# Score tiles of 1024 keys over two PSUM banks in the attention stages of a hybrid block

## The chip, the cores and the metric

One core of one Trainium2 chip runs the whole layer. The metric is the device time of one execution in microseconds (us). Three runs of the kernel before took 2777.36, 2782.47 and 2783.66 us; their median is 2782.47.

## What is computed

One block of a residual trunk over 2048 rows of width 1024, in float32 at both ends: a normalised projection into six parts, differential attention (4 heads of two softmax maps) and stick-breaking attention (8 heads) beside each other, an output projection, and a gated feed-forward part. What the change touches are the two attentions:

```
def diff_attention(q, k, v, lam, rel_bias):       # per block of 128 queries
    logits = einsum('bqhcd,bkhcd->bhcqk', qb, k) * scale + bias     # c = 0, 1: two maps
    p = softmax(where(mask, logits, -inf))
    attn = p[:, :, 0] - lam * p[:, :, 1]
    return einsum('bhqk,bkhd->bqhd', attn, v)

def stick_breaking_attention(q, k, v):            # A[t,s] = beta_ts * prod_{s<j<t}(1 - beta_tj), s < t
    z = einsum('bqhd,bkhd->bhqk', qb, k) * scale
    log_1mb = where(mask, log_sigmoid(-z), 0)
    rem = cumsum(log_1mb, reverse=True) - log_1mb
    a = where(mask, exp(log_sigmoid(z) + rem), 0)
    return einsum('bhqk,bkhd->bqhd', a, v)
```

## The kernel before

The work is cut into 8 groups: groups 0 to 3 are the four heads of differential attention, groups 4 to 7 are pairs of stick-breaking heads. A stream of projections (`proj`, line 379, 16 row tiles a group) runs ahead of the attention of its group, under the attention of the group before, and after the last group comes the output projection (`out_proj`, line 744), which is interleaved with the end of group 7. The feed-forward part follows. `advance` (line 708) sets how far the projections are written ahead. The order of instructions on each engine is not written by hand: a scheduler picks, by priority and by when it expects operands and buffers to be free, and each engine then runs its own list in that order. The attention functions `probs` and `stage_a` have a raised priority (`"at": 200` in line 32).

Scores of a query block (128 queries, index i from 0 to 15) against its (i+1)*128 keys are made in blocks of up to 1024 keys (index b, so two blocks from i = 8 on), and these in pieces of up to 512 keys, the width of one PSUM bank. `score_chunk` (line 446) issues two matmuls per piece into a score tile `sc`, and for the diagonal a third one with a mask (line 450). The pool has four such tiles, one bank each (lines 478 and 552). Two further banks hold the value products `yp`, two the projections `pj`.

Differential attention (`probs`, line 462): for each of two maps m, VectorE copies a piece from PSUM to `z` with scaling and a running maximum (line 483), and for the last 256 keys with the bias added (line 487). Then follow exponentials on ScalarE (line 497), the difference of the maps on VectorE (line 507), and `split_t` (line 398), which splits the weights into two 16-bit halves (a cast and a subtraction, lines 89 or 93 and 98) and transposes them by DMA into `aT`, the input of the value matmuls (`pv`, line 453).

Stick-breaking attention (`stage_a`, line 540) goes through a block from its last piece to its first. For each piece ScalarE writes sigmoid(-z) to `om` (line 554) and sigmoid(z) over the scores in PSUM (line 555); VectorE scans the running product of `om` backwards (line 557), which names the PSUM tile as an operand too, and multiplies sigmoid(z) by the shifted product into `be` (line 558). Only then is the score tile free. A memset (line 545) or a copy of the carry of the block before (line 547) opens each block. `split_t` then casts `be` on ScalarE and subtracts on GpSimd. The profile names `om` and `be` both z. Value matmuls (`stage_b`, line 565) come up to five blocks later.

`transposed` (line 591) uses the same ring of score tiles for transposing rows at the start (line 611) and in the output path (line 782).

## Time and profile before

| | us |
|---|---|
| three runs | 2777.36, 2782.47, 2783.66 |
| profiled execution: span from its first to its last instruction | 2785.0 |
| differential attention (first to last score, some 106 to 616) | 510 |
| stick-breaking attention, first score of group 4 to last scan (616 to 1402) | 786 |
| output path and feed-forward, from some 1400 on | 1385 |

For the profiled execution the profile gives the span and no separate time around it; the span is 2.5 us over the median of the three runs and 1.3 us over the slowest. In rows of groups, a row has the line, engine and operation, the tiles out<-in, the count, then busy us and mean ns of one, then idle us of the engine just before such instructions, with what ended it. Rows of windows give start:end, length, and busy us with counts for PE, PE's weight loads (PEld), DVE (VectorE), ACT (ScalarE) and POOL (GpSimd), then the granted TensorE clock, the DMA share and GB/s.

### The profile page before, as it was taken

How to read it: one execution, taken by the hardware profiler on the slowest of the kernel's cores; microseconds unless marked ns; L12 is line 12 of the kernel's file. 1: busy time of each engine (PE TensorE's matmuls, PEld its weight loads, DVE VectorE, ACT ScalarE, POOL GpSimd, SP SyncE). 2: the span in 40 equal slices, each digit the busy share in tenths (PEclk: the TensorE clock that was granted, in tenths of full speed). 3: DMA queues.
4: the chain of work that ended last, by engine and by line, in shares of the span. 5: the costliest groups of instructions: out<-in, count | busy, mean ns of one | idle time of the engine just before them, and what ended most of it. 6: DMA issues, size and time to landing. Idle time of an engine off the chain costs nothing. (4 is left out here: it accounts for less than half of the span.)

```text
span 2785.0 us, 45469 instructions
## 1 busy us (share of the span) xinstructions
PE 2489.9 (89%) x17084; PEld 1409.0 (51%) x17084; DVE 2000.8 (72%) x3782; ACT 1361.8 (49%) x2543; POOL 1445.2 (52%) x1008
## 2 busy tenths in 40 slices
PE   6998989888878786888889798989999999999998
PEld 4665556555545453557775343444444444444443
DVE  6888879687989989876756877777786644434445
ACT  4665656466878788765644534443442212111121
POOL 2567767665544555546665656565654332322323
PEclk9999999999999897999999999999999999999999
DMA  6788787789999998997796565655658844635534
GB/s 225 199 167 184 147 188 163 164 174 205 198 205 198 192 182 160 190 198 205 197 309 253 184 235 189 221 187 191 240 170 299 327 155 178 227 125 190 211 129 166
DMA packets 649133, 551.91 MB, mean 198 GB/s; under 512 B 506624, under 2 KB 574208, under 8 KB 638672
## 3 DMA queue, kind: packets, MB, share of 16 engines
q1 hardware_dynamic: 647088, 546.92, 71.2%
q8 instruction: 134, 2.20, 0.3%
q0 software_dynamic: 512, 1.36, 0.2%
q10 hardware_dynamic: 1312, 0.72, 0.1%
q14 instruction: 87, 0.71, 0.1%
HBM read 265.27 MB, written 151.52 MB: 150 GB/s over the span
## 5 line engine op out<-in xcount | busy, mean ns | idle before, releaser
L98 POOL TENSOR_TENSOR s<-z,s 128x1024 f16<-128x1024 f32 (+7 forms) x288 | 474.1, 1654 | 334.8 <-ACT s L89 299.3
L320 PE MATMUL pj<-w,xt 128*128 128x384 f16 x3072 | 572.3, 334 | 32.6 <-DVE st L330 11.6
L320 PEld LDWEIGHTS <-xt 128*128 128x128 f16 x3072 | 299.9, 100 | 241.8 <-issue 36.3
L448 PE MATMUL sc<-kT,qT 128*128 128x512 f16 (+3 forms) x1280 | 346.9, 362 | 74.6 <-DVE z L558 34.4
L1034 PE MATMUL pd<-wd,act 128*128 128x512 f16 x1848 | 406.2, 379 | 3.3 <-DVE hs L1040 2.4
L557 DVE TENSOR_TENSOR_SCAN z<-z,sc 128x512 f32<-128x512 f32 (+3 forms) x320 | 355.5, 1112 | 68.6 <-ACT sc L555 65.1
L458 PE MATMUL yp<-v,aT 128*128 128x64 f16 (+1 forms) x4896 | 281.2, 207 | 80.0 <-DMA aT<-s 79.2
L458 PEld LDWEIGHTS <-aT 128*128 128x128 f16 x4896 | 245.2, 102 | 169.4 <-DMA aT<-s 105.1
L936 PEld LDWEIGHTS <-wg 128*128 128x128 f16 x1848 | 183.9, 100 | 264.3 <-issue 58.8
L98 POOL TENSOR_TENSOR hs<-hs,cu 128x512 f32<-128x512 f32 x132 | 170.5, 1297 | 238.2 <-DVE cu L1040 82.6
L936 PEld LDWEIGHTS <-wu 128*128 128x128 f16 x1848 | 181.0, 98 | 222.1 <-issue 9.0
L1034 PEld LDWEIGHTS <-act 128*128 128x128 f16 x1848 | 180.6, 98 | 222.6 <-issue 4.7
L98 POOL TENSOR_TENSOR act<-cg,act 128x512 f16<-128x512 f32 x117 | 160.8, 1385 | 247.7 <-ACT act L992 141.5
L98 POOL TENSOR_TENSOR fst<-fst 128x512 f32<-128x512 f32 x97 | 179.6, 1852 | 167.6 <-DVE wd L215 78.6
L1040 DVE SCALAR_TENSOR_TENSOR hs<-pd,c,hs 128x512 f32<-128x512 f32 x192 | 142.1, 748 | 160.8 <-PE pd L1034 159.1
L89 ACT CAST s<-z 128x384 f16<-128x384 f32 (+7 forms) x216 | 170.1, 788 | 151.5 <-DMA aT<-s 56.4
L554 ACT ACTIVATE z<-sc,c 128x512 f32<-128x512 f32 (+3 forms) x320 | 202.6, 633 | 10.6 <-PE sc L448 6.5
L558 DVE TENSOR_TENSOR z<-sc,z 128x512 f32<-128x512 f32 (+3 forms) x320 | 193.3, 606 | 8.1
L992 ACT CAST act<-cg 128x512 f16<-128x512 f32 x132 | 80.6, 617 | 234.2 <-DVE cg L998 190.9
L555 ACT ACTIVATE sc<-sc,c 128x512 f32<-128x512 f32 (+3 forms) x320 | 194.8, 609 | 0.0
L761 PE MATMUL po<-wo,mt 128*128 128x256 f16 x1536 | 181.3, 276 | 11.0 <-DVE xf L764 6.3
L936 PE MATMUL pm<-X,wg 128*128 128x512 f16 x792 | 179.1, 379 | 1.2 <-ACT bx L1109 1.2
(233 smaller groups left out, 4028.4 us busy)
## 6 DMA issues: line engine op xcount, KB each, us to landing
xt<-xs SPq DMA_DIRECT2D x112, 512.0 KB, 4.4
hs<-hd SPq DMA_DIRECT2D x96, 512.0 KB, 4.3
hd<-hs SPq DMA_DIRECT2D x80, 512.0 KB, 3.2
split<-wg SPq DMA_DIRECT2D x11, 1792.0 KB, 10.5
split<-wu SPq DMA_DIRECT2D x11, 1792.0 KB, 10.3
split<-wd SPq DMA_DIRECT2D x11, 1792.0 KB, 10.4
wg<-split SPq DMA_DIRECT2D x11, 1792.0 KB, 7.3
wd<-split SPq DMA_DIRECT2D x11, 1792.0 KB, 8.4
```

What stands on the lines that cost most here:

```text
L89: ACT.copy(dst, src)
L98: (DVE if e == "D" else POOL).tensor_tensor(dst, a_, b_, op)
L320: PE.matmul(pj[:, :384], lhsT=xv[:, xi, kt, :], rhs=G["w"][:, wi, kt, :], start=n == 0, stop=n == 23)
L448: PE.matmul(sc[:, : 128 * w].rearrange("p (t n) -> p t n", n=P), lhsT=G["q"][i // 4][:, 2 - 2 * o + m, i % 4, :], rhs=G["k"][q][:, m, 0:w, ...
L458: PE.matmul(yp[:, y0 : y0 + wd], lhsT=aT[:, a_, :], rhs=v[:, v_ : v_ + wd], start=start and j == 0 and q == 0, stop=stop and j == nb - 1 a ...
L554: ACT.activation(om[:, lo:hi], sc[:, :w], AF.Sigmoid, scale=G["nkz"][:])
L555: ACT.activation(sc[:, :w], sc[:, :w], AF.Sigmoid, scale=G["kz"][:])
L557: DVE.tensor_tensor_scan(ov, ov, sc[:, :w], om[:, hi : hi + 1], op0=ALU.mult, op1=ALU.bypass)
L558: DVE.tensor_tensor(be[:, lo:hi], sc[:, :w], om[:, lo + 1 : hi + 1], ALU.mult)
L761: PE.matmul(po[:, sl], lhsT=mt[:, kt, P * xi : P * xi + P], rhs=wos[2 * h + n][wi][:, kt, :], start=q == 0, stop=q == 23)
L936: PE.matmul(ps_[:].rearrange("p (t n) -> p t n", n=P), lhsT=wv[:, wo, wi, 128 * kt : 128 * kt + 128], rhs=X[xo][:, :, xi, kt, :], start=st ...
L1034: PE.matmul(po[:], lhsT=act[:, ao, xi, 128 * j : 128 * j + 128], rhs=W["d"][:, wo, wi, :], start=start and u == 0 and q == 0, stop=u == nu ...
```

## The change

The four score tiles of 512 keys become two of 1024 keys, over two banks each (`scores`, a new function of one line). Each piece's matmuls still write one bank. The instructions behind them run once over all keys of a block, up to 1024: in differential attention the scaling with maximum and the biased one, in stick-breaking the two sigmoids, the scan and the product. `transposed` takes a whole two-bank tile and uses its first half. Cut to its core:

```
+            def scores():
+                return ps.tile([P, 1024], F32, tag="sc", bufs=2, name=nm("sc"))
...
-                            z = z4()
+                            z, sc = z4(), scores()
                             for c in range((n + 511) // 512):
                                 lo, hi = 512 * c, min(512 * c + 512, n)
-                                sc = ps.tile([P, 512], F32, tag="sc", bufs=4, name=nm("sc"))
-                                score_chunk(G, sc, i, 2 * b + c, m, (hi - lo) // P)
-                                f = min(max(near - 1024 * b - lo, 0), hi - lo)
-                                note("D", 1.05 * (hi - lo) + 200)
-                                if f > 0:
-                                    DVE.tensor_scalar(z[:, lo : lo + f], sc[:, :f], ...)
...
+                                score_chunk(G, sc[:, lo:hi], i, 2 * b + c, m, (hi - lo) // P)
+                            f = min(max(near - 1024 * b, 0), n)
+                            note("D", 1.05 * n + 200)
+                            if f > 0:
+                                DVE.tensor_scalar(z[:, :f], sc[:, :f], ...)
...
+                            if f < n:
+                                DVE.tensor_tensor_reduce(z[:, f:n], sc[:, f:n], ...)
...
+                    sc = scores()
                     for c in range((n - 1) // 512, -1, -1):
                         lo, hi = 512 * c, min(512 * c + 512, n)
-                        w = hi - lo
-                        sc = ps.tile([P, 512], F32, tag="sc", bufs=4, name=nm("sc"))
-                        score_chunk(G, sc, i, 2 * b + c, m, w // P, b == i // 8 and hi == n)
-                        ACT.activation(om[:, lo:hi], sc[:, :w], AF.Sigmoid, scale=G["nkz"][:])
-                        ACT.activation(sc[:, :w], sc[:, :w], AF.Sigmoid, scale=G["kz"][:])
-                        ov = om[:, lo:hi][:, ::-1]
-                        DVE.tensor_tensor_scan(ov, ov, sc[:, :w], om[:, hi : hi + 1], op0=ALU.mult, op1=ALU.bypass)
-                        DVE.tensor_tensor(be[:, lo:hi], sc[:, :w], om[:, lo + 1 : hi + 1], ALU.mult)
-                        note("A", 1.7 * w + 400)
-                        note("D", 3.15 * w + 350)
+                        score_chunk(G, sc[:, lo:hi], i, 2 * b + c, m, (hi - lo) // P, b == i // 8 and hi == n)
+                    ACT.activation(om[:, :n], sc[:, :n], AF.Sigmoid, scale=G["nkz"][:])
+                    ACT.activation(sc[:, :n], sc[:, :n], AF.Sigmoid, scale=G["kz"][:])
+                    ov = om[:, :n][:, ::-1]
+                    DVE.tensor_tensor_scan(ov, ov, sc[:, :n], om[:, n : n + 1], op0=ALU.mult, op1=ALU.bypass)
+                    DVE.tensor_tensor(be[:, :n], sc[:, :n], om[:, 1 : n + 1], ALU.mult)
+                    note("A", 1.7 * n + 400)
+                    note("D", 3.15 * n + 350)
```

Over the program, line 557's scans go from 320 to 192, as do the products and both sigmoids; line 483's scalings from 256 to 160, line 487's from 152 to 136. Lines of the changed kernel stand two or three higher: sigmoids at 555 and 556, scan at 558, product at 559.

The first place is ScalarE's list in group 6, query block 9, over the two heads' full blocks of 1024 keys: `sc` are score tiles, `z` is `om` in the sigmoids and `be` in the casts, `s` the 16-bit halves, `yrs` and `mo` belong to the end of the blocks before, `st` to the projection. Before:

```order
L554 ACTIVATE z_13845<-sc_13847,c_10728 128x512
L555 ACTIVATE sc_13847<-sc_13847,c_10727 128x512
L554 ACTIVATE z_13845<-sc_13854,c_10728 128x512
L555 ACTIVATE sc_13854<-sc_13854,c_10727 128x512
L148 ACTIVATE yrs_13812<-yss_13809,c_10726 128x8
L327 ACTIVATE st_14861<-pj_14863 128x4x64
L554 ACTIVATE z_13901<-sc_13903,c_10728 128x512
L555 ACTIVATE sc_13903<-sc_13903,c_10727 128x512
L554 ACTIVATE z_13901<-sc_13910,c_10728 128x512
L555 ACTIVATE sc_13910<-sc_13910,c_10727 128x512
L89 CAST s_13835<-z_13824 128x256
L89 CAST s_13861<-z_13844 128x1024
```

The same place in the changed kernel's list of ScalarE, on into the blocks of 384 keys of query block 10:

```order
L555 ACTIVATE z_13235<-sc_13237,c_10328 128x1024
L556 ACTIVATE sc_13237<-sc_13237,c_10327 128x1024
L89 CAST s_13225<-z_13214 128x256
L438 ACTIVATE mo_13210<-yp_12853,c_265 128x4x128
L555 ACTIVATE z_13286<-sc_13288,c_10328 128x1024
L556 ACTIVATE sc_13288<-sc_13288,c_10327 128x1024
L89 CAST s_13246<-z_13234 128x1024
L555 ACTIVATE z_13327<-sc_13329,c_10328 128x384
L556 ACTIVATE sc_13329<-sc_13329,c_10327 128x384
L89 CAST s_13297<-z_13285 128x1024
```

Before, the sigmoids of both heads' four pieces stand ahead of the casts of the blocks before; now the cast of each block stands behind the sigmoids of the next block and ahead of those of the one after.

The second place is VectorE's list in group 5, query block 11, from the blocks of 512 keys into the full ones: `z` is `om` in memset, copy and scan (SCALAR_TENSOR_TENSOR with a score tile is the scan) and `be` in the product, `v` and `st` are outputs of the projections, `m`, `c` and `sW` belong to a weight's scale. Before:

```order
L558 TENSOR_TENSOR z_11726<-sc_11729,z_11727 128x512
L545 MEMSET z_11767 128x1
L178 TENSOR_REDUCE m_13132<-wsc_13128 128x1
L557 SCALAR_TENSOR_TENSOR z_11767<-z_11767,sc_11769 128x512
L195 TENSOR_SCALAR m_13132<-m_13132 128x1
L558 TENSOR_TENSOR z_11766<-sc_11769,z_11767 128x512
L547 COPY z_11792<-z_11727 128x1
L330 SCALAR_TENSOR_TENSOR v_13091<-pj_13092,v_13091 128x2x64
L170 TENSOR_SCALAR c_13127<-m_13132 128x1
L171 TENSOR_SCALAR c_13127<-c_13127 128x1
L557 SCALAR_TENSOR_TENSOR z_11792<-z_11792,sc_11794 128x512
L172 TENSOR_SCALAR c_13126<-c_13127 128x1
```

The same place in the changed kernel's list of VectorE:

```order
L559 TENSOR_TENSOR z_11256<-sc_11259,z_11257 128x512
L547 MEMSET z_11297 128x1
L558 SCALAR_TENSOR_TENSOR z_11297<-z_11297,sc_11299 128x512
L559 TENSOR_TENSOR z_11296<-sc_11299,z_11297 128x512
L549 COPY z_11322<-z_11257 128x1
L558 SCALAR_TENSOR_TENSOR z_11322<-z_11322,sc_11324 128x1024
L559 TENSOR_TENSOR z_11321<-sc_11324,z_11322 128x1024
L549 COPY z_11348<-z_11297 128x1
L558 SCALAR_TENSOR_TENSOR z_11348<-z_11348,sc_11350 128x1024
L559 TENSOR_TENSOR z_11347<-sc_11350,z_11348 128x1024
```

The projection's outputs and the weight's scale, which stood between scan and product here, are gone from this stretch; they stand in the first query blocks of the group.

More of the change, by code (lines that the diff above doesn't have):

```diff
@@ L591, in transposed @@
             def transposed(xn, o):
-                tr = ps.tile([P, 512], F32, tag="sc", bufs=4, name=nm("xtr"))
+                tr = scores()
                 for j in range(4):
                     PE.transpose(tr[:, P * j : P * j + P], xn[:, o + P * j : o + P * j + P], id32[:])
-                return tr
+                return tr[:, :512]
             @pri("fr")
```

11 lines of the change are left out of this document (5 added, 6 removed).

## The prediction, made before the changed kernel ran

> **What bounds the kernel now.** I read the page first (shares, the row of tenths), then the windows by stage, then the waits of each engine in the stick-breaking stage, then the groups by shape, and last the timeline of a stretch of that stage. The page gives the span and the two engines that could bound it:
>
> ```profile
> span 2785.0 us, 45469 instructions
> PE 2489.9 (89%) x17084; PEld 1409.0 (51%) x17084; DVE 2000.8 (72%) x3782; ACT 1361.8 (49%) x2543; POOL 1445.2 (52%) x1008
> ```
>
> The shares are an average over stages. The windows of differential attention (106 to 616 us), of the main part of stick-breaking attention (616 to 1200), of its end (1200 to 1400) and of what follows, with TensorE's (PE) busy time first, VectorE's (DVE) third, ScalarE's (ACT) fourth, and the granted clock behind POOL:
>
> ```profile
> 106.00:616.00 510.00, 463.64 (x3637) 296.16 (x3636) 431.98 (x1304) 306.15 (x796) 353.95 (x253) 0.97 0.80 171
> 616.00:1200.00 584.00, 463.16 (x4761) 291.31 (x4759) 519.30 (x929) 457.11 (x880) 304.51 (x196) 0.93 0.96 192
> 1200.00:1400.00 200.00, 175.29 (x1833) 143.42 (x1832) 141.46 (x233) 121.49 (x212) 112.13 (x76) 0.97 0.79 201
> 1400.00:2785.00 1385.00, 1309.88 (x6407) 627.83 (x6404) 834.00 (x1156) 426.29 (x556) 635.39 (x435) 0.98 0.58 209
> ```
>
> In differential attention TensorE is busy 464 of 510 us (91%) and VectorE 432 (85%): TensorE bounds. From 616 to 1200 it is the other way: VectorE 519 of 584 (89%), idle 65; TensorE 463 (79%). From 1200 on TensorE has 88% and more, and VectorE little to do. So what the change does to VectorE counts in one window of 584 us, and what it does to TensorE's order counts everywhere that scores are made. The waits there, first TensorE's and VectorE's from 616 to 1200 (who waited for whom, us in total, times, longest), then TensorE's of the same kind in the window from 100 to 616:
>
> ```profile
> PE yp L458 <- DMA aT<-s: 41.4, 39, 3.3
> PE sc L448 <- DVE z L558: 32.6, 31, 2.0
> PE sc L448 <- DVE z L545: 16.7, 19, 1.9
> PE sc L448 <- DVE z L547: 8.3, 11, 1.8
> DVE z L557 <- ACT sc L555: 33.5, 41, 3.2
> ...
> PE sc L448 <- DVE mx L487: 0.4, 2, 0.2
> PE sc L448 <- DVE z L483: 0.3, 1, 0.3
> ```
>
> In stick-breaking, TensorE stands 57.6 us before a score matmul until VectorE has read an old score tile to its end: the four PSUM banks for scores are full, and VectorE drains them. In differential attention that wait is 0.7 us: slots are no limit there.
>
> **What the change removes.** The groups by shape in the window 616 to 1200 (count, then busy us and mean ns of one):
>
> ```profile
> L557 DVE TENSOR_TENSOR_SCAN z<-z,sc 128x512 f32<-128x512 f32 x180 | 229.0, 1272 | 20.6 <-ACT sc L555 18.1 <-PE pj L320 1.6 <-PE sc L450 0.4
> L557 DVE TENSOR_TENSOR_SCAN z<-z,sc 128x256 f32<-128x256 f32 x28 | 20.7, 738 | 4.7 <-ACT sc L555 4.5
> L558 DVE TENSOR_TENSOR z<-sc,z 128x512 f32<-128x512 f32 x180 | 123.4, 686 | 4.7
> L558 DVE TENSOR_TENSOR z<-sc,z 128x256 f32<-128x256 f32 x28 | 11.7, 418 | 0.7
> L554 ACT ACTIVATE z<-sc,c 128x512 f32<-128x512 f32 x180 | 125.7, 698 | 4.6 <-PE sc L448 4.0 <-PE sc L450 0.4
> L554 ACT ACTIVATE z<-sc,c 128x256 f32<-128x256 f32 x28 | 13.4, 480 | 0.0
> L555 ACT ACTIVATE sc<-sc,c 128x512 f32<-128x512 f32 x180 | 121.5, 675 | 0.0
> L555 ACT ACTIVATE sc<-sc,c 128x256 f32<-128x256 f32 x28 | 12.8, 455 | 0.0
> L89 ACT CAST s<-z 128x1024 f16<-128x1024 f32 x62 | 65.0, 1049 | 41.2 <-issue 13.1 <-DVE z L558 12.6 <-POOL s L98 11.3
> L89 ACT CAST s<-z 128x640 f16<-128x640 f32 x14 | 10.3, 733 | 3.2 <-DVE z L558 1.2 <-POOL s L98 0.9 <-issue 0.7
> ```
>
> Two widths give a slope and a fixed part. Scan: (1272 - 738)/256 = 2.09 ns an element, 204 ns fixed. Product: 1.05 and 150. Sigmoids: 0.85 and 262, 0.86 and 235. An instruction over 1024 keys, which the trace does not show, is on these lines (an estimate) scan 2.34 us, product 1.22, together 3.56 us against 2 x 1.96 = 3.92; the two sigmoids 2.25 us against 2.75. A merge of two pieces saves VectorE 0.35 us and ScalarE 0.50. How many merges lie in the window:
>
> ```profile
> L557 DVE TENSOR_TENSOR_SCAN z<-z,sc 128x512 f32<-128x512 f32 (+3 forms) x264 | 290.6, 1103 | 37.0 <-ACT sc L555 33.5 <-PE pj L320 1.6 <-PE sc L450 0.4
> L558 DVE TENSOR_TENSOR z<-sc,z 128x512 f32<-128x512 f32 (+3 forms) x264 | 158.3, 601 | 6.8
> L547 DVE COPY z<-z 128x1 f32<-128x1 f32 x48 | 6.8, 141 | 0.0
> L545 DVE MEMSET z<- 128x1 f32 x111 | 6.5, 59 | 0.0
> ```
>
> One copy or memset opens each block: 111 + 48 = 159 blocks in 264 pieces, so 105 merges, and 105 x 0.35 = 37 us off VectorE where it bounds. The other 23 of 128 merges lie past 1200, where TensorE bounds: nothing. ScalarE's 52 us count only through the chain below. Differential attention loses 96 of 256 scalings and 16 of 152 biased ones. Here are the rows of the whole run for the scaling:
>
> ```profile
> L483 DVE TENSOR_SCALAR_CACHE_REDUCE z<-sc,c 128x512 f32<-128x512 f32 x168 | 122.6, 742 | 14.4 <-PE sc L448 12.7 <-POOL s L93 1.0 <-POOL s L98 0.5
> L483 DVE TENSOR_SCALAR_CACHE_REDUCE z<-sc,c 128x256 f32<-128x256 f32 x32 | 15.2, 474 | 0.3 <-PE sc L448 0.3
> L483 DVE DVE_READ_ACCUMULATOR z<-sc,c 128x1 f32 x256 | 20.5, 80 | 0.0
> ```
>
> Fixed part 742 - 2 x 268 = 206 ns, with its accumulator read 0.29 us; 112 x 0.29 = 32 us off VectorE, under TensorE's 91% cover. I count 0, with 15 us of gain at most (half).
>
> **What it adds: a coarser ring.** Keys in flight stay at 2048, but in two slots instead of four, and a slot comes free only when the product over all its keys is done. While VectorE works on one slot, TensorE and ScalarE must fill the other. Rows of the timeline from 1050 to 1085 us, for the parts of such a fill:
>
> ```profile
> 1061.06 0.69 DVE L558 TENSOR_TENSOR z<-sc,z 128x512 f32<-128x512 f32 x1
> ...
> 1061.81 0.61 PE L448 MATMUL sc<-kT,qT 128*128 128x512 f16 x2 [0.65 <-DVE z L558]
> ...
> 1074.19 1.32 PE L448 MATMUL sc<-kT,qT 128*128 128x512 f16 x4 [0.23 <-DVE z L558]
> ...
> 1076.83 1.89 PE L448 MATMUL sc<-kT,qT 128*128 128x512 f16 x4 [1.33 <-DVE z L558]
> ...
> 1078.51 1.49 PE L458 MATMUL yp<-v,aT 128*128 128x64 f16 x24
> ...
> 1081.42 0.39 PE L448 MATMUL sc<-kT,qT 128*128 128x256 f16 x2 [0.99 <-DVE z L547]
> ...
> 1081.65 0.22 PE L450 MATMUL sc<-tri,idb 128*128 128x128 bf16 x1
> ```
>
> The hand-over from product to matmul takes 0.06 us; four matmuls take 1.32, two narrow ones with the mask some 0.45. I walk one cycle by hand at query block 9, whose blocks are F1, F2 (1024 keys, two heads) and p1, p2 (256 keys). The order in the section on the change puts the cast of a block behind the sigmoids of the next one; a cast takes 1.05 us, over 256 keys 0.42 (slope of the two cast rows). At 0 VectorE ends F1 and starts F2, until 3.7. p1 is filled meanwhile (matmuls 0.5, cast of F1 until 1.1, sigmoids 0.94 until 2.05). VectorE does p1 until 4.9 (0.74 + 0.42). But p2 needs the slot that F2 left at 3.7: matmuls until 4.2, cast of F2 until 4.8, sigmoids until 5.75. VectorE idles 0.9, and does p2 until 7.0. The next F1 got p1's slot at 4.9: matmuls until 6.25, sigmoids until 8.5. VectorE idles 1.5. The next F2 is ready in time. The cycle takes 12.25 us; with four slots of 512 it was bound by VectorE alone at 4 x 1.96 + 2 x 1.16 + 0.4 = 10.6. With other VectorE work beside it (519.3 - 448.9 = 70 us in the window, 16% of scan and product, 1.6 us a cycle) it was 12.2. So at block 9 the saving of 0.7 is eaten by 2.4 of gaps, unless other work lies in just these gaps. At block 14 (p of 896 keys) the same walk gives gaps of 0.5. I take 1.6 on average; 48 copies are 24 cycles, so 38 us of gaps, with 0 (all filled) and 58 (2.4 everywhere) as bounds.
>
> Then the fill itself is late: TensorE is in-order, a score matmul stands behind blocks of value or projection matmuls (24 take 1.49 above), and four score matmuls take 1.32 or 1.89. Four slots hid that; with two, fill and drain of a full block are level (0.06 + 1.32 + 2.25 + 0.1 = 3.7 against 3.7), so each delay shows. Bounds 0 (TensorE waits there already) and 0.57 (1.89 - 1.32) on each of 159 blocks, 91 us; nearest row is the wait now, 57.6 us over 264 fills, which says that TensorE is mostly early. I take a quarter of the upper bound, 22 us. In differential attention, where the slot wait is 0.7 us, two slots hold one query block's first scores instead of two or more; I take 4 us, between -15 (the gain above) and 40 (0.2 us, the wait per fill in the later stage, on its 192 blocks). The transposes at lines 592 and 781 use the same ring, one slot each; 0.
>
> Sum against the profiled execution's span: -37 + 38 + 22 + 0 + 4 = +27, 2785 + 27 = 2812. The three runs' median lies 2.5 us under that span (2782.47); taken off, 2809.
>
> By the Trainium skill (Perfetto Trace Analysis, Optimizing Tensor Performance) matmul groups should rotate through PSUM banks so that one bank's draining lies beside the next group's matmuls, which speaks against fewer, wider slots; the rows of slot waits here bear it out. The same page (Optimizing Scalar/DVE Operations) says that grouping into larger operations helps an engine that is saturated, and gives an overhead of about 125 ns for a VectorE instruction on PSUM; with two per merge that would be an estimate of 26 us in place of the 37 from the rows.
>
> **The rivals.** *Grouping wins.* VectorE is the bound, other work fills the gaps (70 us of it are there, 38 of gaps), TensorE keeps waiting early. Then -37 remains, with ScalarE's shorter sigmoids taking nothing more: 2785 - 37 - 2.5 = 2745. For it: 57.6 us of slot waits now, so fills have slack. Against it: in the changed order long runs of VectorE have nothing but copy, scan and product, so the other work is not where the gaps are. It decides if VectorE's idle time in this stage stays under 65 + 37 = 102 us. The rule on grouping just cited is this rival. Chance 0.27.
>
> *Head of line on TensorE.* Score matmuls that wait for one of two slots hold value and projection matmuls behind them, in differential attention too, where TensorE is the bound: +27 - 4 + 40, and the later stage's delay at 0.3 us per block (48 instead of 22): 2785 + 89 - 2.5 = 2872. Against it: 0.7 us of slot wait now. Chance 0.07.
>
> *It cancels.* Gaps and delays come to 37: 2782. Chance 0.08. That the merge does not happen is excluded: the order shows 192 scans instead of 320.
>
> **How the numbers follow.** My forecast, slower at 2809, has the remaining 0.58; with its terms at half and at double strength it spans 2785 to 2850. The range reaches down into the grouping case and up to the edge of the head-of-line case: 2755 to 2855, with 0.12 below and 0.08 above. Slower by over 0.2% (5.6 us, about what a measurement of this kernel can tell from no change): 0.58 + 0.07 = 0.65; within it 0.08; faster 0.27.
>
> **What would show it.** Right: VectorE's busy time in stick-breaking falls by some 37 us, while "scan waits for sigmoid" grows from 33.5 us to 80 or more, and the sigmoids' wait for score matmuls grows too; a scan of 1024 takes 2.34 us, a product 1.22. Differential attention keeps its length within 10 us. Wrong: the scan's waits stay near 33 us and the stage ends earlier; or score matmuls wait for VectorE in differential attention; or the time is lost past 1400 us, where the change has no instruction but the transposes of the output path.

## The result, and the profile after

The changed kernel takes 2883.72 us (median of 4 runs, 2875.77 to 2887.26), the kernel before 2783.06 (4 runs, 2777.36 to 2785.41): a ratio of 1.0366, 95% interval 1.0349 to 1.0383. It is slower, as forecast, but by 101 us instead of 27, and above the range's upper end of 2855. The span and the engines' shares, from the page of the changed kernel:

```profile
span 2883.3 us, 44612 instructions
PE 2536.5 (88%) x17084; PEld 1429.9 (50%) x17084; DVE 1972.2 (68%) x3305; ACT 1331.9 (46%) x2288; POOL 1436.4 (50%) x1004
```

VectorE works less (1972 against 2001 us) and the span is longer, so the loss is idle time. The windows say in which stage. Those of the kernel before, cut at the first and the last score work of each stage (columns as in the prediction):

```profile
106.00:614.00 508.00, 462.13 (x3612) 294.67 (x3610) 430.01 (x1295) 304.17 (x793) 353.95 (x253) 0.97 0.80 171
614.00:1403.00 789.00, 642.96 (x6641) 438.91 (x6642) 665.62 (x1175) 581.93 (x1096) 418.77 (x273) 0.94 0.92 194
1403.00:2785.00 1382.00, 1306.88 (x6379) 625.14 (x6377) 831.10 (x1152) 424.93 (x553) 633.26 (x434) 0.98 0.58 209
```

And those of the changed kernel at the same places of the program:

```profile
116.00:622.00 506.00, 460.48 (x3624) 296.47 (x3620) 410.13 (x1087) 303.18 (x791) 344.89 (x251) 0.97 0.79 172
622.00:1500.00 878.00, 678.60 (x6649) 456.44 (x6648) 650.45 (x904) 549.20 (x833) 411.18 (x268) 0.87 0.81 173
1500.00:2883.00 1383.00, 1306.39 (x6312) 619.83 (x6308) 832.28 (x1149) 424.01 (x553) 632.39 (x434) 0.98 0.58 208
```

Differential attention keeps its length (508, 506), what follows stick-breaking too (1382, 1383). The first window begins 10 us later, of which 2 are won back in it; the stick-breaking window grows from 789 to 878. There VectorE's busy time falls by 15 us, and its idle time (length less busy) rises from 123 to 228, by 104. The granted clock falls from 0.94 to 0.87.

In the rows of single instructions the saving is there. Scan, product and sigmoids over 1024 keys, and the two lines as a whole, from the groups of the changed kernel:

```profile
L558 DVE TENSOR_TENSOR_SCAN z<-z,sc 128x1024 f32<-128x1024 f32 x80 | 187.6, 2344 | 68.0 <-ACT sc L556 61.5 <-PE pj L323 2.2 <-PE yp L461 0.5
L559 DVE TENSOR_TENSOR z<-sc,z 128x1024 f32<-128x1024 f32 x80 | 97.5, 1219 | 2.4
L555 ACT ACTIVATE z<-sc,c 128x1024 f32<-128x1024 f32 x80 | 89.2, 1115 | 54.6 <-PE sc L451 53.8 <-PE yp L461 0.3
L556 ACT ACTIVATE sc<-sc,c 128x1024 f32<-128x1024 f32 x80 | 86.8, 1085 | 0.0
...
L558 DVE TENSOR_TENSOR_SCAN z<-z,sc 128x128 f32<-128x128 f32 (+7 forms) x192 | 330.7, 1723 | 148.7 <-ACT sc L556 135.6 <-PE pj L323 2.2 <-PE yp L461 1.3
L559 DVE TENSOR_TENSOR z<-sc,z 128x128 f32<-128x128 f32 (+7 forms) x192 | 174.4, 908 | 6.5 <-DVE z L558 0.5
```

The same two lines of the kernel before, whole run:

```profile
L557 DVE TENSOR_TENSOR_SCAN z<-z,sc 128x512 f32<-128x512 f32 (+3 forms) x320 | 355.5, 1112 | 68.6 <-ACT sc L555 65.1 <-PE pj L320 1.6 <-PE sc L450 0.4
L558 DVE TENSOR_TENSOR z<-sc,z 128x512 f32<-128x512 f32 (+3 forms) x320 | 193.3, 606 | 8.1
```

By these rows scan and product together fall from 548.8 to 505.1 us, 44 less, of which only 15 arrive in VectorE's busy time (why is said further down), and the scan's wait for its sigmoid doubles (65.1 to 135.6). That wait, followed backwards through the waits of the stick-breaking stage, first before:

```profile
PE yp L458 <- DMA aT<-s: 51.6, 50, 3.3
PE sc L448 <- DVE z L558: 34.4, 33, 2.0
PE sc L448 <- DVE z L545: 18.1, 20, 1.9
PE sc L448 <- DVE z L547: 9.0, 12, 1.8
DVE z L557 <- ACT sc L555: 65.1, 55, 7.2
ACT z L554 <- PE sc L448: 6.5, 9, 2.2
ACT z L554 <- PE sc L450: 2.5, 3, 1.7
```

and then in the changed kernel:

```profile
PE yp L461 <- DMA aT<-s: 89.8, 66, 3.7
PE sc L451 <- DVE z L547: 52.9, 35, 4.3
PE sc L451 <- DVE z L549: 18.6, 16, 3.2
DVE z L558 <- ACT sc L556: 135.6, 80, 8.8
ACT z L555 <- PE sc L451: 71.8, 58, 4.8
ACT z L555 <- PE sc L453: 20.0, 16, 3.9
```

The sigmoids now wait 92 us for score matmuls (9 before), and TensorE itself waits 90 us (52 before) for transposed weights `aT` in front of value matmuls. The waits for a slot (52.9 + 18.6 = 71.5 us) have hardly grown from 34.4 + 18.1 + 9.0 = 61.5. One such place in the changed kernel's timeline:

```profile
1005.45 1.23 DVE L559 TENSOR_TENSOR z<-sc,z 128x1024 f32<-128x1024 f32 x1
...
1007.38 0.85 PE L461 MATMUL yp<-v,aT 128*128 128x64 f16 x21 [3.07 <-DMA aT<-s]
...
1008.04 1.04 PE L451 MATMUL sc<-kT,qT 128*128 128x512 f16 x2
...
1010.08 1.11 ACT L555 ACTIVATE z<-sc,c 128x1024 f32<-128x1024 f32 x1 [2.28 <-PE sc L451]
...
1012.21 2.35 DVE L558 TENSOR_TENSOR_SCAN z<-z,sc 128x1024 f32<-128x1024 f32 x1 [1.76 <-ACT sc L556]
```

A product ends at 1006.68 and frees its slot. TensorE comes to the next score matmuls only at 1008.04: value matmuls stood in front of them, and those had waited 3.07 us for a DMA, until 1007.38. The sigmoid starts at 1010.08, 3.40 us after the slot was free, and VectorE has by then nothing left: it idles 1.76 us before the scan.

I took this distance for all blocks of the stage, the start of the first sigmoid less the end of the product two blocks back: over the 80 full blocks it is 4.19 us in the mean (median 2.55, longest 21.8), where the prediction walked 0.06 + 1.32 = 1.4. Over 190 blocks the distances sum to 724 us (3.8 each). The larger part of them, 410 us, passes before the block's first score matmul starts: 2.16 us in the mean (median 0.96), and over 1 us for 94 of the 190 blocks. Within the 724 us TensorE is busy 636: 212 with score matmuls and 36 with their masks, but also 204 with projections, 144 with the output projection and 111 with value matmuls (these overlap a little, so the parts come to more than the whole).

### The profile page after: what moved, and what is told of

Same layout as the page of the kernel before. It is cut to its first block, busy times and chain, and to the rows that moved or that the text cites. A ratio compares the mean times of both kernels' runs of the same rounds, so it can differ in the third digit from the quotient of the medians.

```text
span 2883.3 us, 44612 instructions
## 1 busy us (share of the span) xinstructions
PE 2536.5 (88%) x17084; PEld 1429.9 (50%) x17084; DVE 1972.2 (68%) x3305; ACT 1331.9 (46%) x2288; POOL 1436.4 (50%) x1004
## 5 line engine op out<-in xcount | busy, mean ns | idle before, releaser
L98 POOL TENSOR_TENSOR s<-z,s 128x1024 f16<-128x1024 f32 (+7 forms) x288 | 466.1, 1625 | 396.9 <-ACT s L89 379.2
L323 PE MATMUL pj<-w,xt 128*128 128x384 f16 x3072 | 565.1, 336 | 24.0 <-DMA xt<-xs 7.1
L558 DVE TENSOR_TENSOR_SCAN z<-z,sc 128x128 f32<-128x128 f32 (+7 forms) x192 | 330.7, 1723 | 148.7 <-ACT sc L556 135.6
L451 PE MATMUL sc<-kT,qT 128*128 128x512 f16 (+3 forms) x1280 | 331.0, 379 | 81.3 <-DVE z L547 52.9
L461 PE MATMUL yp<-v,aT 128*128 128x64 f16 (+1 forms) x4896 | 267.4, 213 | 117.2 <-DMA aT<-s 116.9
L451 PEld LDWEIGHTS <-qT 128*128 128x128 f16 x1280 | 116.4, 103 | 187.0 <-DVE z L547 66.1
L555 ACT ACTIVATE z<-sc,c 128x128 f32<-128x128 f32 (+7 forms) x192 | 166.3, 866 | 92.8 <-PE sc L451 71.8
L559 DVE TENSOR_TENSOR z<-sc,z 128x128 f32<-128x128 f32 (+7 forms) x192 | 174.4, 908 | 6.5 <-DVE z L558 0.5
```

What stands on the lines that cost most here:

```text
L98: (DVE if e == "D" else POOL).tensor_tensor(dst, a_, b_, op)
L323: PE.matmul(pj[:, :384], lhsT=xv[:, xi, kt, :], rhs=G["w"][:, wi, kt, :], start=n == 0, stop=n == 23)
L451: PE.matmul(sc[:, : 128 * w].rearrange("p (t n) -> p t n", n=P), lhsT=G["q"][i // 4][:, 2 - 2 * o + m, i % 4, :], rhs=G["k"][q][:, m, 0:w, ...
L461: PE.matmul(yp[:, y0 : y0 + wd], lhsT=aT[:, a_, :], rhs=v[:, v_ : v_ + wd], start=start and j == 0 and q == 0, stop=stop and j == nb - 1 a ...
L555: ACT.activation(om[:, :n], sc[:, :n], AF.Sigmoid, scale=G["nkz"][:])
L558: DVE.tensor_tensor_scan(ov, ov, sc[:, :n], om[:, n : n + 1], op0=ALU.mult, op1=ALU.bypass)
```

## The experiments

Two theories. **LATE**: TensorE, which is in-order, reaches the score matmuls late, behind value matmuls that wait for `aT`, projections and output matmuls; four slots hid that, and two have no reserve. **FILL**: the loss is in the wide slot itself; hand-over, four matmuls and two wide sigmoids are no shorter than the drain of the other slot, however early TensorE comes.

**Which stage.** `sb_only` has the wide tiles in stick-breaking alone, `diff_only` in differential attention alone (with the transposes of that time); the score pools are opened one after the other:

```
+                if g == 4:
+                    rescore()      # closes the score pool, opens one of the other shape
```

> Only stick-breaking attention (and the transposes of the output path) uses the two wide slots; differential attention and the transposes at the start keep four slots of 512 keys. If the loss is all in stick-breaking: its span of 788 us grows to some 876 as in the changed kernel, and the total is 2865 to 2880 us (the 8 us at the start and in differential attention gone). Rival (the two stages push each other, as projections of the next group are laid differently): well under 2850 us.

> Only differential attention and the transposes at the start use the two wide slots; stick-breaking keeps four of 512. TensorE bounds that stage, so VectorE's saved 32 us buy nothing and the 60 us that scalings waited for scores cost little: 2780 to 2795 us. Rival (head of line on TensorE there): 2800 us or more.

Measured: `sb_only` 2866.19 us, 1.0300 (1.0283 to 1.0318); `diff_only` 2783.87, 1.0006 (0.9993 to 1.0020). Most of the loss belongs to stick-breaking, and both times lie in the bands given first. Merging 112 instructions in differential attention, where TensorE bounds, is worth nothing and costs nothing in the total. The stages trade time, though: in `diff_only` the first score comes 10 us later than before, differential attention takes 9 us longer, and stick-breaking with its old slots takes 761 us instead of 786. So a difference of some 20 us in the length of a single stage says little.

**How many slots.** `ring3_512` is the kernel before with one change, at all three places that take a score tile:

```
-                        sc = ps.tile([P, 512], F32, tag="sc", bufs=4, name=nm("sc"))
+                        sc = ps.tile([P, 512], F32, tag="sc", bufs=3, name=nm("sc"))
```

> The kernel before with three narrow slots instead of four. LATE: each slot fewer takes reserve against TensorE's delays, so a loss between none and that of two narrow pieces in flight (3028 us in ring2_narrow): 2830 to 2930 us. Rival (only the wide instructions hurt): 2783 to 2800 us.

Measured: 2846.25 us, 1.0232 (1.0208 to 1.0256). One narrow slot less, with no wide instruction anywhere, costs some 64 us: within LATE's band.

Two experiments put narrow instructions into wide slots. `ring2_narrow` in both attentions:

```
-                    sc = scores()
+                    sc2 = scores()
                     for c in range((n - 1) // 512, -1, -1):
                         lo, hi = 512 * c, min(512 * c + 512, n)
+                        sc = sc2[:, lo:hi]
...
+                        (matmuls, sigmoids, scan, product of this piece, as before)
```

> Two score slots of two banks as in the change, but all instructions over 512 keys as before (nothing is left out of the computation). Theory FILL (a whole slot must be filled by wide sigmoids, 3.7 us, under the drain of one other slot): narrow pieces let the first scan start some 2.1 us after a slot is free, so the gaps go, 2785 to 2815 us. Rival HOLD (two slots that come free only after the last product are too few, whatever the width): 2860 us and more, since the 46 us of saved fixed cost are lost too. Rival WIDTH (the wide instructions and the order they give put TensorE behind value matmuls that wait for transposes): 2783 us, and the wait of value matmuls for aT back from 117 to some 80 us.

Measured: 3028.11 us, 1.0887 (1.0870 to 1.0903), in the band of HOLD. It does not tell the theories apart, because fewer keys are in flight than intended. Its timeline (here the product of a first piece, the opening of the next block, and the matmuls of the second piece):

```profile
1140.54 0.69 DVE L562 TENSOR_TENSOR z<-sc,z 128x512 f32<-128x512 f32 x1
...
1141.14 0.14 DVE L550 COPY z<-z 128x1 f32<-128x1 f32 x1
1141.28 1.01 PE L451 MATMUL sc<-kT,qT 128*128 128x512 f16 x2 [1.03 <-DVE z L550]
```

The matmuls into the second bank start only when the product on the first is done: in this kernel the dependency goes by the tile, not by the half of it. Over the whole stage no piece's matmuls start before the product two pieces back has ended, so two pieces of 512 are in flight instead of four. That costs 245 us, and with `ring3_512` it is a series: four, three and two narrow pieces take 2783, 2846 and 3028 us.

`ring2_first` mends this in stick-breaking: all score matmuls of a block first, then sigmoids, scan and product piece by piece.

```
                         score_chunk(G, sc2[:, lo:hi], i, 2 * b + c, m, (hi - lo) // P, ...)
+                    for c in range((n - 1) // 512, -1, -1):
+                        lo, hi = 512 * c, min(512 * c + 512, n)
+                        sc = sc2[:, lo:hi]
+                        (sigmoids, scan, product of this piece, as before)
```

> In stick-breaking all score matmuls of a block are issued first into the two-bank slot, then sigmoids, scan and product run over 512 keys each as before; differential attention is as in the changed kernel. Theory FILL (what hurts is the 2.2 us of two wide sigmoids before the first scan may start): the first scan can start 0.9 us earlier, gaps mostly go, 2785 to 2830 us. Theory LATE: the slots are as few and TensorE as late, and the 46 us of fixed cost are back: 2870 to 2930 us.

Measured: 2941.6 us, 1.0584 (1.0558 to 1.0609), 12 us above LATE's band and far from FILL's. Its scan:

```profile
L562 DVE TENSOR_TENSOR_SCAN z<-z,sc 128x512 f32<-128x512 f32 (+3 forms) x320 | 356.8, 1117 | 192.0 <-ACT sc L560 179.6 <-PE yp L434 5.6 <-PE yp L461 0.9
```

The first scan of a block could now start after two narrow sigmoids, and still the waits for sigmoids rise to 179.6 us. At two slots wide instructions are 58 us better than narrow ones, so it is not the wide instructions that cost.

To have a third wide slot at all, `psj` and `yp` give up one bank each. Three kernels at that price: three wide slots, two wide slots, four narrow ones (the kernel before).

```
-        psj = top.enter_context(tc.tile_pool(name="psj", bufs=2, space=PSUM, side="right"))
+        psj = top.enter_context(tc.tile_pool(name="psj", bufs=1, space=PSUM, side="right"))
...
-                        ypd[i // k] = ps.tile([P, 512], F32, tag="yp", name=nm("yp"))
+                        ypd[i // k] = ps.tile([P, 512], F32, tag="yp", bufs=1, name=nm("yp"))
...
-                return ps.tile([P, 1024], F32, tag="sc", bufs=2, name=nm("sc"))
+                return ps.tile([P, 1024], F32, tag="sc", bufs=3, name=nm("sc"))
```

> The changed kernel with a third wide score slot. The two banks come from the value products and the projections, which keep one bank each in the attention stages (in the feed-forward part the eight banks are shared out as 7 and 1 instead of 6 and 2). Theory LATE (TensorE comes late to the score matmuls, in median 2.55 us and in mean 4.2 us after a slot is free, and two slots hold no reserve against it): at least 60 us under the run with two wide slots and one bank each (wide2_one), and the scans' wait for sigmoids under 80 us. Rival ORDER (wide instructions as such make a worse list): within 20 us of wide2_one.

> Control for the run above: the changed kernel with one bank each for value products and projections, two banks left unused, two wide slots. Both theories: 2884 us or more, since it has the same slots and less of the rest.

> Control: the kernel before with one bank each for value products and projections, two banks left unused, four narrow slots. It prices the lost banks with the old instructions: 2783 us if they cost nothing, up to 2830 us if projections and value products then wait for their readers. Three wide slots beat the old ring at equal banks if wide3_one is under this run.

Measured, beside 2778.73 us for the kernel before on that chip: `wide3_one` 3002.55, 1.0805 (1.0778 to 1.0832); `wide2_one` 3093.92, 1.1134 (1.1109 to 1.1158); `narrow4_one` 3035.46, 1.0926 (1.0897 to 1.0955). The scans of the three, in this order:

```profile
L558 DVE TENSOR_TENSOR_SCAN z<-z,sc 128x128 f32<-128x128 f32 (+7 forms) x192 | 330.7, 1722 | 127.2 <-ACT sc L556 114.9 <-PE sc L451 2.5
```

```profile
L558 DVE TENSOR_TENSOR_SCAN z<-z,sc 128x128 f32<-128x128 f32 (+7 forms) x192 | 330.8, 1723 | 198.9 <-ACT sc L556 185.6 <-PE sc L451 4.0
```

```profile
L557 DVE TENSOR_TENSOR_SCAN z<-z,sc 128x512 f32<-128x512 f32 (+3 forms) x320 | 356.0, 1115 | 93.2 <-ACT sc L555 87.1 <-PE yp L458 1.8 <-PE yp L431 1.1
```

The third wide slot alone, with everything else equal, gains 91 us, and the scan's waits for sigmoids fall by 71. LATE had asked for 60 us and more, which holds, and for waits under 80 us, which does not (114.9). Three wide slots beat four narrow ones by 33 us, but they also hold six banks of keys against four; six narrow slots were not tried, so this is not the worth of merging alone. The two banks given up cost 257 us over all stages where at most 47 were expected, so no kernel of this kind can win here.

**A shorter fill, with two wide slots.** `early_wide` writes the second sigmoid to `be` in SBUF, so that the slot is free after the sigmoids and not after the product:

```
-                    ACT.activation(sc[:, :n], sc[:, :n], AF.Sigmoid, scale=G["kz"][:])
+                    ACT.activation(be[:, :n], sc[:, :n], AF.Sigmoid, scale=G["kz"][:])
...
-                    DVE.tensor_tensor_scan(ov, ov, sc[:, :n], ...)
-                    DVE.tensor_tensor(be[:, :n], sc[:, :n], om[:, 1 : n + 1], ALU.mult)
+                    DVE.tensor_tensor_scan(ov, ov, be[:, :n], ...)
+                    DVE.tensor_tensor(be[:, :n], be[:, :n], om[:, 1 : n + 1], ALU.mult)
```

> The changed kernel, but the second sigmoid writes to the SBUF tile be, and scan and product read it there, so a score slot is free once ScalarE has read it (same computation). FILL and HOLD: the slot is held 3.7 us instead of 7.3 or more, the next block is filled while VectorE drains, the gaps of 135 us before scans fall under 60 and the saved fixed cost of 46 us shows: 2730 to 2790 us. WIDTH: the same wide instructions stand in the same kind of order: 2850 us or more.

Measured: 2936.63 us, 1.0556 (1.0541 to 1.0572). The 2730 to 2790 us of FILL and HOLD are missed; the time lies in WIDTH's band, but for a reason that no theory had. Its groups, over 1024 keys and as a whole, with GpSimd's subtraction last:

```profile
L558 DVE TENSOR_TENSOR_SCAN z<-z,z 128x1024 f32<-128x1024 f32 x80 | 216.7, 2709 | 16.7 <-ACT z L556 16.2
L559 DVE TENSOR_TENSOR z<-z,z 128x1024 f32<-128x1024 f32 x80 | 152.7, 1910 | 0.7
L558 DVE TENSOR_TENSOR_SCAN z<-z,z 128x128 f32<-128x128 f32 (+7 forms) x192 | 393.8, 2054 | 31.0 <-ACT z L556 30.0
L559 DVE TENSOR_TENSOR z<-z,z 128x128 f32<-128x128 f32 (+7 forms) x192 | 286.6, 1496 | 4.9 <-issue 1.3 <-DVE c L311 0.3
L98 POOL TENSOR_TENSOR s<-z,s 128x1024 f16<-128x1024 f32 (+7 forms) x288 | 587.6, 2051 | 277.5 <-ACT s L89 217.4 <-issue 17.3 <-DVE z L559 10.8
```

The scan's wait does go (135.6 to 30.0 us). But with both operands in SBUF scan and product take 680 us instead of 505, 175 more than in the changed kernel, and the whole loses. A VectorE that drains so much more slowly waits less by that alone, so this run does not show what the earlier release is worth.

**TensorE made early.** LATE says that a TensorE that comes early to the scores makes two wide slots cheap. Three pairs, each of the kernel before and the changed one. `light` cuts the matmuls of projections, values and output to a third, by leaving out the two correction terms of each product; `nowait` gives value matmuls a constant operand that is always there instead of the weights, so that its result is not the layer's; `free` has both.

```
-                    for xi, wi in ((0, 0), (0, 1), (1, 0)):
+                    for xi, wi in ((0, 0),):
...
-                        PE.matmul(yp[:, y0 : y0 + wd], lhsT=aT[:, a_, :], ...)
+                        PE.matmul(yp[:, y0 : y0 + wd], lhsT=id16[:], ...)
```

> The kernel before with TensorE's other matmuls cut to a third: projections, value products and output projection keep only the first of their three half-precision products (the two small correction terms are left out; score matmuls and everything on VectorE and ScalarE stay). It is the base for after_light: VectorE bounds stick-breaking alone, and the total falls by 100 us or more.

> The changed kernel with the same correction terms left out. Theory LATE (between a slot's release and its first sigmoid TensorE runs 470 us of projection, output and value matmuls that stand ahead of the scores): with a third of them left the loss of 100 us against its base shrinks to 30 us or less, or turns into a gain of up to 37 us as grouping alone would give. Rival (fill of two wide sigmoids, or order of wide instructions): the difference to before_light stays 80 us or more.

> Base for the next run: the kernel before, but the value matmuls read a constant identity tile instead of the transposed weights aT, in the same number (the transposes still run, nothing waits for them; the attention outputs are then not the reference's). Here TensorE loses only its 80 us of waits for transposes, most of them while VectorE is the bound: 2730 to 2783 us.

> The changed kernel with the same constant in place of aT. Theory LATE, with the wait for transposes as one of its parts (117 us in the changed kernel against 79): the difference to before_nowait falls from 100 to some 50 to 75 us, since projection and output matmuls still stand ahead of scores. Rival (waits for transposes only fill time in which the slot is held anyway): 95 us or more remain.

> Base for the next run: the constant in place of aT, and the correction terms of projections, value products and output projection left out as in before_light. TensorE is then mostly free ahead of every score: 2650 to 2711 us.

> The changed kernel with both. Theory LATE: nothing long stands ahead of the scores any more, the loss is gone, between -37 us (grouping alone) and +20 us against before_free. Rival FILL (two wide sigmoids and block sizes that alternate leave gaps of their own): +30 to +60 us remain. Rival ORDER (nothing to do with TensorE): +80 us or more.

| pair | before, us (ratio, interval) | changed, us (ratio, interval) | loss, us |
|---|---|---|---|
| as it is | 2783.06 | 2883.72 (1.0366, 1.0349 to 1.0383) | 101 |
| light | 2711.26 (0.9744, 0.9721 to 0.9768) | 2774.23 (0.9977, 0.9967 to 0.9987) | 63 |
| nowait | 2777.41 (0.9982, 0.9971 to 0.9993) | 2826.90 (1.0158, 1.0140 to 1.0177) | 49 |
| free | 2718.16 (0.9769, 0.9754 to 0.9783) | 2759.54 (0.9920, 0.9896 to 0.9944) | 41 |

Ratios are to the kernel before as it is; the loss is the difference of the pair. Half of it goes with the wait for `aT` alone: 49 us are left, just under the 50 to 75 that LATE expected. To the kernel before that wait is worth 0.2%, some 5 us: four slots hide it almost wholly, two don't. Fewer matmuls take away 38 us, between the numbers of the two theories; both together take away 60, so the parts overlap, and 41 stay, outside LATE's band and in the band given to FILL. Two of the bases missed their numbers: `before_light` fell by some 70 us and not by 100 or more, and `before_free` stayed 7 us above its band. The scan in `after_nowait`, then in `after_free`:

```profile
L558 DVE TENSOR_TENSOR_SCAN z<-z,sc 128x128 f32<-128x128 f32 (+7 forms) x192 | 330.7, 1722 | 108.7 <-ACT sc L556 98.9 <-PE sc L453 1.0
```

```profile
L558 DVE TENSOR_TENSOR_SCAN z<-z,sc 128x128 f32<-128x128 f32 (+7 forms) x192 | 330.7, 1722 | 89.8 <-ACT sc L556 79.6 <-DVE z L549 0.5 <-DVE z L547 0.5
```

A likely reason why `light` kept more of the loss than `nowait`: its value matmuls wait 185 us for `aT` over the whole run, 117 in the changed kernel:

```profile
L461 PE MATMUL yp<-v,aT 128*128 128x64 f16 (+1 forms) x1632 | 138.6, 235 | 186.2 <-DMA aT<-s 185.0 <-DVE mo L439 0.5
```

What is left in `free` is seen in its stick-breaking windows, first of `before_free`:

```profile
580.00:1341.00 761.00, 436.60 (x2688) 212.61 (x2688) 661.88 (x1127) 568.08 (x1057) 413.65 (x272) 0.69 0.86 187
```

then of `after_free`, with a stretch of its timeline:

```profile
577.00:1387.00 810.00, 432.66 (x2694) 221.38 (x2694) 640.78 (x871) 532.46 (x793) 409.27 (x266) 0.67 0.81 176
```

```profile
902.80 1.89 PE L451 MATMUL sc<-kT,qT 128*128 128x512 f16 x4 [1.10 <-DVE z L549]
...
903.86 2.35 DVE L558 TENSOR_TENSOR_SCAN z<-z,sc 128x1024 f32<-128x1024 f32 x1 [1.06 <-ACT sc L556]
...
904.72 1.11 ACT L555 ACTIVATE z<-sc,c 128x1024 f32<-128x1024 f32 x1
...
906.24 1.22 DVE L559 TENSOR_TENSOR z<-sc,z 128x1024 f32<-128x1024 f32 x1
```

TensorE is busy 433 of 810 us and now waits for the slot, as it should. But the granted clock is 0.67, four score matmuls take 1.89 us, and the distance from a free slot to its first sigmoid is 2.09 us in the median of the full blocks. With the sigmoids' 2.09 that makes a fill of 4.2 us against a drain of 3.68: at this clock the wide slot is late by about half a microsecond even when nothing stands ahead of it, more than the 0.35 us that the merge saves. VectorE's idle time rises by 70 us within this pair (99 to 169), against 104 as it is. `nowait` shows the same 70 (112 to 182), with a granted clock of 0.87 like that of the changed kernel as it is, so the low clock of `free` is not needed for it. Nor is TensorE always early in `after_free`: its first score matmul starts 0.06 us after the slot is free in the median, but over 1 us after it for 42 of 190 blocks, 216 us in all. So the 70 us are FILL's at most, and some of LATE may still be in them.

**The transposes in the ring.** `transposed` takes a whole wide slot for half of it, and the output path of the blocks before runs within stick-breaking. In this pair it takes a bank of `psj` instead, in both kernels:

```
-                tr = scores()
+                tr = psj.tile([P, 512], F32, tag="pj", name=nm("xtr"))
```

> Control for the run above: the kernel before with the transposes in the projections' banks. Nothing or a small loss where projections and transposes now share two banks: 2780 to 2800 us.

> The changed kernel with the transposes at the start and in the output path moved from the score ring to the projections' banks, so that a transposed row half no longer takes one of the two wide slots. If the loss in the last stick-breaking group (295 us against 266) and at the start (8 us) comes from that: 2845 to 2865 us. Rival (it comes from output matmuls ahead of scores): 2875 us or more.

Measured: `before_trpj` 2873.88 us, 1.0329 (1.0311 to 1.0348); `after_trpj` 2951.80, 1.0607 (1.0585 to 1.0630). The control misses its 2780 to 2800 us: the projection's banks can't spare this, and it costs the kernel before 93 us. So the time of `after_trpj`, above the rival's 2875, does not speak for the rival either. The difference within the pair is 78 us instead of 101, so the shared ring could explain some 20 us at most; with projections disturbed as well, that stays open.

## Why the prediction was wrong

**The saving was right for one instruction and too large for the stage.** Scan 2.34 us forecast and 2344 ns measured, product 1.22 and 1219, the two sigmoids 2.25 together and 1115 + 1085. By their rows scan and product lost 44 us over the whole stage, where 37 were forecast for the merges up to 1200. But the sign that the prediction named was VectorE's busy time, and that fell by 15 us (21 in the pair `free`). The rows of neighbouring instructions overlap: before the change the product that starts at 1061.06 ends at 1061.75, and the next scan starts at 1061.67. Counted once where they overlap, scan and product together take 534 us before and 505 after, 29 less, and other VectorE work overlapped with them more before than after. The lower estimate that the prediction set beside its 37, 26 us, was nearer. The other sign held: the scan's wait for sigmoids had to grow from 33.5 to 80 us or more, and over the stage's first three groups it grew from 30 to 93.

**Differential attention was right.** 508 to 506 us for a forecast of 4 us, and `diff_only` shows nothing. VectorE's waits for scores do grow there, from 18.7 us to this row of the changed kernel, and TensorE's 91% covers them:

```profile
DVE z L485 <- PE sc L451: 49.8, 35, 6.1
```

**The failed step is the price of having two slots: gaps (38 us) and late fills (22 us), 60 together.** VectorE's idle time in the stage rose by 104. With the saving at 15 instead of 37, the stage lost 89 us (-15 + 104) where the prediction had 23 (-37 + 60). Most of the rest lies at the start, where the transposes were put at 0 and the first score comes 10 us later; `sb_only`, which keeps the old slots there, starts at 106 us as before.

*Late fills.* "Nearest row is the wait now, 57.6 us over 264 fills, which says that TensorE is mostly early. I take a quarter of the upper bound, 22 us." The rows say otherwise: by their counts the 57.6 us are 31 + 19 + 11 = 61 waits, so for three quarters of the fills TensorE did not stand before a full ring. How late it came to those, the wait cannot say, and four slots covered it. In the kernel before, too, a slot's first sigmoid started 5.3 us in the mean after the slot had come free (316 pieces, four pieces back; ScalarE's own queue is in it), under the cover of three other slots with a drain of 3 x 1.96 = 5.9 us. With two slots the cover is one drain of 3.7. The 0.57 us a block of the upper bound stood for one slow batch of score matmuls; the projections, output and value matmuls within the distances alone came to 459 us on 190 blocks, 2.4 each. In the sum the bound of 91 us was not passed: with TensorE relieved, 60 of the 101 us of loss go, and 40 of the 89 in the stage itself (789 to 878 us as it is, 761 to 810 in `free`). It was the quarter that was too little.

*Gaps of a coarse ring* were forecast at 38 us, with 58 as the bound. In `after_free` VectorE's idle time still rises by 70 us, over the bound, though late fills are not wholly gone from it. The walk had fill and drain level at 3.7 us; at the granted clock of that run the fill is longer. How much of the 104 us in the changed kernel is gaps and how much late fills is therefore known only roughly.

**The clock** was no term at all. In the windows above the granted clock goes with how busy TensorE is: 0.94, 0.87 and 0.67 for 81%, 77% and 53%. No run changed the clock by itself. What it does is seen in the time from one score matmul over 512 columns to the next, from start to start: 217 ns in the median before and in the changed kernel (266 and 277 in the mean), but 426 in `after_free` (372 in the mean; 400 and 345 in `before_free`). So it cost the score matmuls little in the changed kernel, by an estimate 7 us (640 matmuls of 11 ns more), and much in the pair `free`. The Trainium skill (TensorE: Matmul & The Clock Gate, Part 1: The HAM clock gate) says that the array's clock is gated to half after an idle window and released by activity, with 426.7 ns from start to start of a matmul over 512 columns when cold and 215.7 when warm; the medians of 426 and 217 agree with that.

**The rivals.** "Head of line on TensorE" came near in the number (2872) and in the mechanism, but the number was partly luck: 40 of its us lay in differential attention, which lost nothing. It had a chance of 0.07. What speaks for it was on the page of waits: 41.4 us of value matmuls waiting for `aT`, in front of score matmuls. I quoted that row and gave it no part in the sum. "Grouping wins" named its own test, VectorE's idle time under 102 us up to 1200; it came to 127 in the first three groups of the stage alone (53 before).

**What stays open.** Of the last 41 us, by the ends of the products in `free`, the first three groups of stick-breaking lose 26 us (531 against 504.5 us) and the last one 22 (278.8 against 256.6), of which 3 come back because the changed kernel of this pair starts the stage earlier. In the last group output matmuls run beside the scores; whether it is they, the shared ring, or the low clock was not separated. No kernel here that computes the whole layer beats the kernel before; `diff_only` equals it.

## What to carry to other kernels

Merging two pieces into one instruction halves the number of slots if the buffer stays the same size, and the slots are what hides an in-order engine's other work. Before such a change, measure for each slot how long after its release the refill is used, and compare that with the drain of the slots that would be left; the total of slot waits does not show it. Take the saving from the engine's busy time, with overlapping rows counted once, and not from single rows (15 us here instead of 44). A merge needs slots to spare: a third wide slot gained 91 us over two. In a stage that another engine bounds it was worth 0 us.

## What was not expected of the hardware

With both operands in SBUF, VectorE's instructions ran longer beside GpSimd's subtractions: the product over 1024 keys 1910 ns instead of 1219, the scan 2709 instead of 2344, and the subtractions themselves 2051 ns in the mean against this row of the changed kernel:

```profile
L98 POOL TENSOR_TENSOR s<-z,s 128x1024 f16<-128x1024 f32 (+7 forms) x288 | 466.1, 1625 | 396.9 <-ACT s L89 379.2 <-issue 5.2 <-DMA xcd<-x 2.8
```

The trace of `early_wide` shows that it is GpSimd's work beside them, and not the place of the operands alone. Two products over 1024 keys, the first with GpSimd's subtractions beside it and the second with none:

```profile
1012.52 10.74 POOL L98 TENSOR_TENSOR s<-z,s 128x1024 f16<-128x1024 f32 x3
...
1014.08 3.13 DVE L559 TENSOR_TENSOR z<-z,z 128x1024 f32<-128x1024 f32 x1
...
1027.26 1.19 DVE L559 TENSOR_TENSOR z<-z,z 128x1024 f32<-128x1024 f32 x1
```

Of the 80 such products, the 19 without a GpSimd row beside them take 1212 ns in the mean, the 50 with one for over half of their time 2249; scans take 2342 (16 of them) and 2902 (42). GpSimd's subtractions over 1024 keys take 2217 ns without a scan or product beside them and 2793 with one (GpSimd's rows are rough). In the changed kernel, where one operand is the score tile in PSUM, the products take 1219 ns without and 1220 with GpSimd beside them. The Trainium skill (SBUF — State Buffer, SBUF: two separate sides) describes a shared port pair of VectorE and GpSimd that is locked for a whole instruction, by a VectorE operation with two SBUF inputs against a GpSimd one that reads SBUF; both sides getting longer, and only beside each other, agrees with that.
